# A two-layer decoder trunk: weight rounding by GpSimd copies, probability scaling by ScalarE, the first layer's gate summed by adding DMAs, and one longer list of steps

## The chip, the core and the metric

The kernel runs on one core of a Trainium2 chip. The core has a matrix engine (TensorE, PE in the profile, with its weight loads as PEld), a vector engine (VectorE, DVE), an engine for activations and scaled copies (ScalarE, ACT), a general engine (GpSimd, POOL), and a queue that mostly issues transfers (SyncE, SP). Each engine works through its own list of instructions in order and waits on semaphores for the others. The metric is the time of one execution on the device in microseconds, less is better. Three runs of the kernel before took 427.09, 427.12 and 428.16 us, median 427.12.

## The reference, cut to what matters

One sequence of 256 tokens of width 1024 passes two layers. Each layer normalizes its input, shifts and scales it with numbers computed from a conditioning vector `c`, applies a mixer, and adds the projected result back, multiplied by a gate that is also computed from `c`:

```
shift, scale, gate = split(c @ ada_w + ada_b)
x = x + gate * mixer(rmsnorm(x) * (1 + scale) + shift)
```

Layer 0 is sparse attention with 16 heads in 4 groups of keys. With 256 tokens all four blocks of 64 are selected, so the selected and the sliding branch are both plain causal attention, on different keys and values, beside a branch on 15 compressed tokens:

```
p   = exp(s - max) / sum;        s = q k^T / 8 - slope * distance
o   = g0 * o_cmp + g1 * o_slc + g2 * o_win
y   = (o * silu(z)) @ w_out
```

Layer 1 is a chunkwise mLSTM with 8 heads, followed by its own output projection and a final norm. Matrix products are made at more than one pass of reduced precision: every float32 operand is split into a rounded part (`hi`) and the remainder (`lo`), and three products hi*hi, hi*lo and lo*hi are added.

## The kernel before, in words

Weights stream from HBM through a ring of ten buffers named `raw`, 128 x 1024 floats each, always loaded on SP's queue and always in the order in which they will be used (`stream_rest`, line 935, fixes that order; a load waits until its buffer's last reader is done). A weight block is then split by two instructions: `make_hi` (line 144) rounds it into a buffer `wh` by a ScalarE copy (line 164), and `make_lo` (line 167) writes the remainder into `wl` by a VectorE subtraction (line 169). There are six pairs of `wh` and `wl`. Blocks of the attention's z path are rearranged on the way, and so take two instructions of 512 elements each for hi and again for lo.

The work has three stages. The first makes the modulated input and the query projection (line 442). The second is the one that the change rewrites: the key, value and gate-logit projections (lines 548 to 550 and 1611 to 1613), the compression network (line 581), the attention itself, the output projection (line 878, named `out_mm`), and the turn to the next layer, in which the residual is added, normalized, transposed and modulated and the first products of layer 1 begin (line 1167). The third is layer 1, whose instructions a scheduler orders.

In the second stage the order is written out by hand. The keys run as a plain loop over the eight blocks of the contraction (`nsa`, line 552), in each block all three kinds of columns. The attention follows a list of steps, `ORDER` (line 613): each word emits the instructions of one step, on whichever engines they run. There are eight units n = 0 to 7 (a pair of key groups, one head of each). `S:n,a` makes the scores of token half a on TensorE, `m:n,a` subtracts distances and takes minima on VectorE, `e:n,a` is the exponential on ScalarE with its sums, `f:n` makes the factors gate/sum on VectorE. Then the probabilities are multiplied by these factors, in eight instructions a unit (`scaled`, line 803): `p:n,j` puts four of them on GpSimd, `s:n,j` four on VectorE, `q:n,j` two on each. `T:n,j,br` transposes them on TensorE, `t:n,j,br` copies the transposes out of PSUM by ScalarE, and `V:n` multiplies by the values. `hi` and `lo` split the next weight block, `z:n,q` are the z path's products, `out:k` and the later `last` calls are the output projection, and `d:s,n` is a VectorE reduction that makes a shift or scale column of layer 1. The turn (line 1092) is straight code behind the list.

The gate of layer 0, a row of 1024 numbers, is made in the list too. `gr:n` runs 16 matmuls of `c` against 512 columns of the gate's weights, four at a time in column groups of 32 (line 226), `gc` copies the result out by ScalarE, `gs` adds the four partial rows and spreads the sum over 128 partitions by one float32 matmul (line 868), and `ga` adds it to the bias by VectorE (line 872).

## Time and profile before

| what | value |
|---|---|
| median of three runs | 427.12 us (427.09 to 428.16) |
| span of the profiled execution, first to last instruction | 425.8 us |
| median of the runs above that span | 1.3 us |
| TensorE busy | 415.7 us, 98% |
| VectorE busy | 353.7 us, 83% |
| ScalarE busy | 272.0 us, 64% |
| GpSimd busy | 82.1 us, 19% |
| granted TensorE clock, mean | 0.999 |
| moved by DMA | 94.54 MB, mean 222 GB/s |

The second stage starts at 52.7 us with the first key product and ends at about 184.8 us with the last products of the turn. A busy time is the union of an engine's instructions. TensorE's instructions overlap in the profile (one starts while the one before is still draining), so a column that says 280 ns for a matmul is not the pace: the pace is read from the starts in the timeline.

### The profile page before, as it was taken

What the parts mean: (1) busy time and instruction counts of PE and PEld (TensorE: products, weight loads), DVE (VectorE), ACT (ScalarE), POOL (GpSimd) and SP (SyncE); (2) the same over time, 40 slices, a digit from 0 to 9 for tenths busy, and PEclk for the clock granted to TensorE, in tenths of its full rate; (3) what the DMA queues carried; (4) which work ended last, traced back from release to release, by engine and by line L of the source; (5) the groups of instructions that cost most, each with busy time, mean ns of one, the idle gap of its engine ahead of it and who ended that gap; (6) DMA issues with size and microseconds to landing.
All of it is one profiled execution on the core that took longest, in us unless ns stands there. A gap on an engine that the chain in (4) does not pass through costs nothing.

```text
span 425.8 us, 7641 instructions
## 1 busy us (share of the span) xinstructions
PE 415.7 (98%) x2701; PEld 359.7 (84%) x2701; DVE 353.7 (83%) x747; ACT 272.0 (64%) x542; POOL 82.1 (19%) x127
## 2 busy tenths in 40 slices
PE   7999999999999999999999999999999999999994
PEld 4899998789778878888998899888888888888884
DVE  6999798999999998979983796889878997458553
ACT  5766693788978964668576865465456454555523
POOL 4000212364586740120000000000000350220000
PEclk9999999999999999999999999999999999999999
DMA  8999986973799678148754366558555687540002
GB/s 313 413 408 407 396 306 192 357 280 107 256 353 391 226 255 307 58 145 295 247 172 168 105 237 190 166 174 264 163 188 197 213 290 229 168 142 0 2 0 99
DMA packets 26886, 94.54 MB, mean 222 GB/s; under 512 B 3072, under 2 KB 3088, under 8 KB 26848
## 3 DMA queue, kind: packets, MB, share of 16 engines
q1 hardware_dynamic: 26208, 92.30, 61.6%
q0 software_dynamic: 352, 0.97, 0.7%
q10 hardware_dynamic: 288, 0.79, 0.5%
q8 instruction: 21, 0.34, 0.3%
q14 instruction: 17, 0.14, 0.1%
HBM read 93.00 MB, written 1.05 MB: 221 GB/s over the span
## 4 chain that ended last, share of the span: by engine, by line
PE 86%; issue 6%; DMA 2%; POOL 2%; DVE 2%; ACT 1%; SPq 1%; DVEq 0%; POOLq 0%; ACTq 0%
PE bank L550 10%; PE bank L548 10%; PE bank L549 10%; PE bank L442 8%; PE bank L1613 6%; PE bank L1611 6%; PE bank L1612 6%; PE bank L1524 5%; PE bank L1045 5%; PE bank L1167 3%; DMA Q<-in_columns 2%; PE bank L808 2%; PE bank L1404 2%; PE bank L825 2%; PE bank L763 2%
## 5 line engine op out<-in xcount | busy, mean ns | idle before, releaser
L169 DVE TENSOR_TENSOR wl<-raw,wh 128x1024 fp32r<-128x1024 f32 (+4 forms) x127 | 139.3, 1112 | 37.3 <-ACT wh L164 36.4
L164 ACT ACTIVATE wh<-raw 128x1024 fp32r<-128x1024 f32 (+4 forms) x127 | 119.4, 957 | 72.9 <-PE bank L550 31.8
L548 PE MATMUL bank<-wh,one 128*128 128x512 f32 (+1 forms) x208 | 76.8, 370 | 0.0
L549 PE MATMUL bank<-wl,one 128*128 128x512 f32 (+1 forms) x208 | 76.3, 367 | 0.0
L550 PE MATMUL bank<-wh,one 128*128 128x512 f32 (+1 forms) x208 | 76.3, 368 | 0.0
L1611 PE MATMUL bank<-one,wh 128*128 128x256 f32 x208 | 59.6, 287 | 0.0
L1613 PE MATMUL bank<-one,wl 128*128 128x256 f32 x208 | 59.2, 285 | 0.1
L1612 PE MATMUL bank<-one,wh 128*128 128x256 f32 x208 | 59.0, 284 | 0.0
L803 POOL TENSOR_SCALAR Pr<-Pr,f 128x128 f32<-128x128 f32 (+1 forms) x42 | 46.7, 1130 | 31.4 <-DVE f L797 25.1
L548 PEld LDWEIGHTS bank<-wh,one 128*128 128x128 f32 x208 | 39.2, 189 | 6.1 <-DVE tz L520 0.2
L550 PEld LDWEIGHTS bank<-wh,one 128*128 128x128 f32 x208 | 39.2, 188 | 6.1
L549 PEld LDWEIGHTS bank<-wl,one 128*128 128x128 f32 x208 | 39.2, 189 | 5.9
L1611 PEld LDWEIGHTS bank<-one,wh 128*128 128x128 f32 x208 | 39.7, 191 | 1.3 <-issue 0.8
L1613 PEld LDWEIGHTS bank<-one,wl 128*128 128x128 f32 x208 | 39.7, 191 | 0.5 <-DVE wl L169 0.3
L1612 PEld LDWEIGHTS bank<-one,wh 128*128 128x128 f32 x208 | 39.7, 191 | 0.1
L789 ACT ACTIVATE Pr<-Pr,mn 128x128 f32<-128x128 f32 (+1 forms) x64 | 28.2, 444 | 4.4 <-DVE mn L782 4.4
L442 PE MATMUL bank<-one,wh 128*128 128x256 f32 x224 | 29.8, 284 | 0.7 <-ACT one L416 0.4
L442 PEld LDWEIGHTS bank<-one,wh 128*128 128x128 f32 x224 | 28.1, 192 | 1.1 <-ACT one L416 0.6
L1487 POOL DMA_DIRECT2D DT<-in_final_g x1 | 0.6, 560 | 131.7 <-DVE pl L1399 131.7
L160 POOL TENSOR_TENSOR raw<-raw,gate 128x256 f32<-128x256 f32 x16 | 15.5, 976 | 47.8 <-DMA raw<-in_out_b 22.5
L1385 DVE SCALAR_TENSOR_TENSOR conv<-bank,one,conv 128x255 f32<-128x255 f32 (+2 forms) x48 | 20.2, 471 | 2.1 <-ACT conv L1380 2.1
L861 DVE CUSTOM_DVE_ANT_0 raw<-raw,one,one 128x1024 f32<-128x1024 f32 x16 | 21.1, 1331 | 0.0
(343 smaller groups left out, 813.6 us busy)
## 6 DMA issues: line engine op xcount, KB each, us to landing
raw<-in_wide SPq DMA_DIRECT2D x44, 512.0 KB, 4.1
raw<-in_units SPq DMA_DIRECT2D x18, 512.0 KB, 3.5
raw<-in_turn SPq DMA_DIRECT2D x16, 512.0 KB, 7.7
raw<-in_gates SPq DMA_DIRECT2D x16, 512.0 KB, 4.7
raw<-in_out_b SPq DMA_DIRECT2D x16, 512.0 KB, 3.8
raw<-in_start SPq DMA_DIRECT2D x8, 512.0 KB, 9.6
Q<-in_columns SPq DMA_DIRECT2D x8, 512.0 KB, 9.6
raw<-in_hidden SPq DMA_DIRECT2D x8, 512.0 KB, 4.2
```

The source lines that it names most:

```text
L164: self.nc.scalar.activation(v(hi), src, AF.Copy)
L169: self.nc.vector.tensor_sub(v(lo), src, v(hi).bitcast(F32))
L442: nc.tensor.matmul(out, w[:, ch * P : ch * P + P], h[:, kk], start=(kk == 0 and m == 0 and ch % 2 == 0), stop=(kk == 7 and m == 2), skip_g ...
L548: nc.tensor.matmul(out, self.hh[:, kk, sl], wh, start=first, stop=False, skip_group_check=True)
L549: nc.tensor.matmul(out, self.hh[:, kk, sl], wl, start=False, stop=False, skip_group_check=True)
L550: nc.tensor.matmul(out, self.hl[:, kk, sl], wh, start=False, stop=last, skip_group_check=True)
L789: nc.scalar.activation(v, v, AF.Exp, bias=mn[:, a, br, j : j + 1], scale=-1.0, accum_out=sm[:, a, br, j : j + 1])
L803: es[br].tensor_scalar(v, v, F[n][:, a, br, j : j + 1], None, op0=OP.mult)
L1045: ins = nc.tensor.matmul(out, l[:, sl], w[:, c0:c1], start=(k == 0 and m == 0), stop=(k == N - 1 and m == 2), skip_group_check=True)
L1611: nc.tensor.matmul(out, wh, self.hh[:, kk], start=first, stop=False, skip_group_check=skip)
L1612: nc.tensor.matmul(out, wh, self.hl[:, kk], start=False, stop=False, skip_group_check=skip)
L1613: nc.tensor.matmul(out, wl, self.hh[:, kk], start=False, stop=last, skip_group_check=skip)
```

## The change

Five things change in the second stage, and the rest only follows.

- Twenty-two of the roundings (`make_hi`) become GpSimd copies: a step `hp` in the list (`np` in the turn) does what `hi` does, on GpSimd. The z path's weights are laid out beforehand so that each block needs one copy and one subtraction instead of two of each.
- The multiplication of probabilities by their factors leaves GpSimd: of 64 such instructions 54 are ScalarE copies with a scale, and 10 stay on VectorE (steps `saa`, `sva`, `sav`, a letter for each branch).
- The gate of layer 0 no longer uses matmuls of `c`. Each of eight blocks of 128 x 1024 weights is multiplied in place by the matching column of `c` on ScalarE (`gm:k`), and a DMA issued by GpSimd adds it into the tile `gate0`, which starts as zeros with the bias in one partition (`gp`). One float32 matmul by ones for each half (`gs:n`, same size as before) then sums over the partitions, and ScalarE copies the result over `gate0` (`ga:n`).
- The keys' columns are three parts, and keys, attention and turn are one list.
- The order of the loads on SP's queue follows the new list: eight loads of one gate block each replace two groups of four.

```diff
-    def make_hi(self, m):
+    def make_hi(self, m, pool=False):
-        if kind == "z":
-            r4 = raw.rearrange("p k j (i d) -> p k j i d", i=2)
-            views = [... two of 512 elements ...]
-        elif kind == "q":
+        if kind == "q":
...
         for v, src in views:
-            self.nc.scalar.activation(v(hi), src, AF.Copy)
+            if pool:
+                self.nc.gpsimd.tensor_copy(v(hi), src)
+            else:
+                self.nc.scalar.activation(v(hi), src, AF.Copy)
...
+        self.gate0 = self.T(pc, [P, D], tag="gate")
+        g.memset(self.gate0, 0.0)
...
             if kk == 2:
+                nc.gpsimd.dma_start(self.gate0[0:1], self.t["ada_b"][0:1, 2048:3072])
...
-        def kv_block(kk):
-            wh, wl = self.take()
+        def kv_block(kk, part):
+            while len(kw) <= kk:
+                kw.append(self.take())
...
         def scaled(n, j, *es):
             for br in range(2):
                 for a in range(2):
-                    v = probs(n, j, br, a)
-                    es[br].tensor_scalar(v, v, F[n][:, a, br, j : j + 1], None, op0=OP.mult)
+                    v, f = probs(n, j, br, a), F[n][:, a, br, j : j + 1]
+                    if es[br] is nc.scalar:
+                        copy(v, v, scale=f)
+                    else:
+                        es[br].tensor_scalar(v, v, f, None, op0=OP.mult)
...
-        def rows(what, n, bank):
-            b = self.bank(bank)
-            B.setdefault("ada", []).append(b)
-            self.ada_rows(b, self.take_raw(4))
...
-        def gate_sum(bank):
-            b = B["gs"] = self.bank(bank)
-            nc.tensor.matmul(b, self.sel, W["A"].pop(0), start=True, stop=True)
+        def gate_sum(n):
+            b = B["gs"] = self.bank(4)
+            nc.tensor.matmul(b, self.ones1.to_broadcast([P, P]), self.gate0[:, 512 * n : 512 * n + 512], start=True, stop=True)
+
+        def gate_copy(n):
+            copy(self.gate0[:, 512 * n : 512 * n + 512], B["gs"])
...
+    def gate_product(self, kc):
+        raw = self.gate_raw = self.take_raw(1, True)[0]
+        self.nc.scalar.activation(raw, raw, AF.Copy, scale=self.pca[:, kc : kc + 1])
+
+    def gate_part(self):
+        self.nc.gpsimd.dma_start(self.gate0, self.gate_raw, accum_op=OP.add)
+        self.used.add(self.kept)
...
     ORDER = """
-    d:0,0 hidden:0 hi hidden:1 S:0,0 lo S:0,1 hi hidden:2 hidden:3 z:0,0 m:0,0 m:0,1 e:0,0 lo S:1,0 ...
+    k:0,1 hi qa:3 lo hi lo k:0,0 k:0,2 k:1,0 hp hi hp k:1,2 qa:1 lo lo k:1,1 k:2,1 k:2,0 hi k:3,0 k:4,0 ...
```

What the new list does to three engines' instructions is shown by pieces of their order. TensorE first: in the middle of the attention before (unit 3 and 4; `bank` tiles are PSUM banks, `raw` the weight blocks, `one_39` holds `c`, `one_16` the identity for transposes, `KH` and `KL` the split keys) the gate's matmuls stand between transposes and scores, followed by a transpose and the gate's sum.

```order
L808 MATMUL bank_1600<-one_16_87,Pr_1349 128x128 x3
L226 MATMUL bank_1615<-raw_1147,one_39_144 32x512
L226 MATMUL bank_1615<-raw_1149,one_39_144 32x512
L226 MATMUL bank_1615<-raw_1151,one_39_144 32x512
L226 MATMUL bank_1615<-raw_1207,one_39_144 32x512
...
L766 MATMUL bank_1624<-KH_758,Q_949 128x256
```

And on TensorE now, in the output projection (`wh` and `wl` are split weight blocks, `Q` the split mixer output, `gate` the tile that the DMAs add into):

```order
L896 MATMUL bank_2041<-wh_1931,Q_1000 128x512
L896 MATMUL bank_2041<-wl_1932,Q_1000 128x512
L896 MATMUL bank_2041<-wh_1931,Q_1000 128x512
L887 MATMUL bank_2271<-gate_134,one_14_85 128x512
L896 MATMUL bank_2040<-wh_2066,Q_1000 128x512
L896 MATMUL bank_2040<-wl_2067,Q_1000 128x512
```

The 16 narrow matmuls are gone from TensorE, the two sums stay, and they have moved from the middle of the attention into the output projection, behind the eighth adding DMA.

GpSimd before, in the middle of the attention (`Pr` are probabilities, `f` the factors):

```order
L803 TENSOR_SCALAR Pr_1193<-Pr_1193,f_1290 128x128
L803 TENSOR_SCALAR Pr_1193<-Pr_1193,f_1290 128x256
L803 TENSOR_SCALAR Pr_1194<-Pr_1194,f_1290 128x128
L803 TENSOR_SCALAR Pr_1194<-Pr_1194,f_1290 128x256
...
L803 TENSOR_SCALAR Pr_1348<-Pr_1348,f_1461 128x128
L803 TENSOR_SCALAR Pr_1348<-Pr_1348,f_1461 128x256
```

GpSimd now, in the same part of the program (the `wh` of `raw_1153` is the last z block, those behind it belong to the output projection):

```order
L1037 DMA gate_134<-raw_1063 128x1024
L165 CAST wh_1417<-raw_1153 128x1024
L1037 DMA gate_134<-raw_1155 128x1024
L165 CAST wh_1498<-raw_1209 128x1024
L1037 DMA gate_134<-raw_1193 128x1024
L165 CAST wh_1610<-raw_1258 128x1024
L165 CAST wh_1748<-raw_1409 128x1024
```

GpSimd's queue now alternates between the weight copies, which VectorE's subtractions and then TensorE wait for, and the adding DMAs, each of which waits for the one before it, since all write the same tile.

ScalarE now, at unit 5 and 6 (`PT` are the copied transposes, `sm` sums, `mn` minima; line 662 is the plain copy, line 818 the exponential, line 1034 the gate's product):

```order
L662 ACTIVATE PT_1922<-bank_1902 128x384
L662 ACTIVATE Pr_1783<-Pr_1783,f_1868 128x128
L662 ACTIVATE Pr_1783<-Pr_1783,f_1868 128x256
L1034 ACTIVATE raw_1480<-raw_1480,one_8_70 128x1024
L662 ACTIVATE PT_1929<-bank_1918 128x384
L662 ACTIVATE Pr_1784<-Pr_1784,f_1868 128x128
L662 ACTIVATE Pr_1784<-Pr_1784,f_1868 128x256
```

ScalarE before, between the same kinds of work:

```order
L633 ACTIVATE PT_2022<-bank_1989 128x384
L164 ACTIVATE wh_2041<-raw_1865 128x1024
L633 ACTIVATE Q_839<-y_327_1637 128x512
L164 ACTIVATE wh_2069<-raw_1867 128x1024
L633 ACTIVATE PT_2092<-bank_2012 128x384
```

Where copies of transposes stood between weight roundings, they now stand between scalings of probabilities and the gate's products.

378 lines of the change are left out of this document (164 added, 214 removed).

## The prediction

> **What bounds the kernel now.** I read the page's busy times first, then the chain that ended last, then the busy times by stage.
>
> ```profile
> PE 415.7 (98%) x2701; PEld 359.7 (84%) x2701; DVE 353.7 (83%) x747; ACT 272.0 (64%) x542; POOL 82.1 (19%) x127
> PE 86%; issue 6%; DMA 2%; POOL 2%; DVE 2%; ACT 1%; SPq 1%; DVEq 0%; POOLq 0%; ACTq 0%
> ```
>
> TensorE is busy for 98% of the span and carries 86% of the chain. So an edit counts in two ways: by what it takes off TensorE's list, and by any wait that it puts in front of TensorE. The table by stage (busy us, number of instructions in brackets, clock, DMA share, GB/s) shows where that holds. The second stage is the first five rows.
>
> ```profile
> core 0: us, PE busy (x) PEld busy (x) DVE busy (x) ACT busy (x) POOL busy (x), PEclk, DMA share, GB/s
> 52.70:80.00 27.30, 27.18 (x216) 23.63 (x216) 25.50 (x50) 19.97 (x43) 4.64 (x8) 1.00 0.78 267
> 80.00:110.00 30.00, 30.00 (x269) 25.31 (x265) 28.52 (x110) 24.58 (x81) 18.21 (x26) 1.00 0.61 224
> 110.00:140.00 30.00, 30.00 (x238) 24.54 (x235) 29.65 (x101) 24.37 (x75) 19.60 (x19) 1.00 0.92 349
> 140.00:160.00 20.00, 19.79 (x133) 15.40 (x132) 19.89 (x37) 15.85 (x36) 10.91 (x7) 1.00 0.75 239
> 160.00:184.80 24.80, 24.00 (x129) 19.74 (x128) 21.16 (x46) 13.63 (x28) 3.41 (x14) 1.00 0.48 172
> ```
>
> The stage takes 132.1 us. TensorE idles 0.12 + 0.21 + 0.80 = 1.1 us in it, at full clock. VectorE is nearly as full: from 80 to 160 us it is busy 78.06 of 80. ScalarE is busy 84.8 of the 107.3 us up to 160, so it idles 22.5. Idle by this table is not all that TensorE loses, since a matmul that starts late still overlaps its predecessor's draining. The timeline (start, duration, engine) shows both kinds:
>
> ```profile
> 55.17 0.28 PE L1611 MATMUL bank<-one,wh 128*128 128x256 f32 x1
> 55.29 0.28 PE L1612 MATMUL bank<-one,wh 128*128 128x256 f32 x1
> 55.69 0.39 PE L1613 MATMUL bank<-one,wl 128*128 128x256 f32 x1
> ...
> 181.67 0.97 PE L1167 MATMUL bank<-wh,one 128*128 128x272 f32 x5 [0.51 <-DVE one L1154]
> ```
>
> The second of these starts 0.12 us after the first, which is the usual pace, but the third 0.40 after the second, so 0.28 is lost without a gap being shown. Altogether little is lost: shortening the waits can bring one or two microseconds, and the rest must come from TensorE's work.
>
> **The change part by part.** *TensorE.* The chain in order of time has the pace of each kind of matmul (start, length, count):
>
> ```profile
> 103.55 2.75 PE bank L825 x32
> ...
> 106.82 0.48 PE bank L830 x4
> ...
> 107.59 0.68 PE bank L808 x6
> 108.28 1.85 PE bank L226 x16
> ...
> 111.13 0.98 PE bank L868 x2
> ...
> 112.44 0.92 PE bank L763 x4
> ...
> 120.06 1.85 PE bank L226 x16
> ```
>
> L226 is the gate by matmuls of `c`: two groups of 1.85 us, 3.7 us in all, and both vanish. The two sums (L868, about 0.98 us each) stay, with other operands of the same type and size. All other matmuls and transposes are the same in number and shape, only in another order. So TensorE sheds 3.7 us. For the change of neighbours (a transpose beside a product, a narrow beside a wide one) I take nothing, between -1 and +1 us.
>
> *VectorE.* These groups (count, busy us, mean ns) change:
>
> ```profile
> L803 DVE TENSOR_SCALAR Pr<-Pr,f 128x256 f32<-128x256 f32 x11 | 4.4, 400 | 0.0
> L803 DVE TENSOR_SCALAR Pr<-Pr,f 128x128 f32<-128x128 f32 x11 | 3.9, 355 | 0.1
> L872 DVE TENSOR_TENSOR gate<-gate,bank 128x512 f32<-128x512 f32 x2 | 1.3, 674 | 0.0
> L169 DVE TENSOR_TENSOR wl<-raw,wh 128x512 fp32r<-128x512 f32 x20 | 13.2, 702 | 0.0
> L169 DVE TENSOR_TENSOR wl<-raw,wh 128x1024 fp32r<-128x1024 f32 x88 | 108.3, 1236 | 37.2 <-ACT wh L164 36.4
> L169 DVE TENSOR_TENSOR wl<-raw,wh 128x816 fp32r<-128x816 f32 x10 | 10.0, 1005 | 0.1
> ```
>
> Of 22 scalings 10 stay: 6 x (0.400 + 0.355) = 4.5 us less. The two additions to the gate go: 1.3 less. The z path's 16 halves of 0.702 become 8 whole subtractions of 1.236: 11.2 - 9.9 = 1.3 less. VectorE sheds 7.2 us (4.5 + 1.3 + 1.3, before rounding). This is what makes the 3.7 us of TensorE collectable: from 80 to 160 us VectorE had only 1.9 us of idle time, less than 3.7, and would have set the pace; now it has 1.9 + 7.2 - 3.7, about 5.4.
>
> *ScalarE.* The roundings that leave it, and the nearest rows for what comes:
>
> ```profile
> L164 ACT ACTIVATE wh<-raw 128x1024 fp32r<-128x1024 f32 x88 | 92.4, 1056 | 70.2 <-PE bank L550 31.8 <-PE bank L1612 13.5 <-DMA raw<-in_start 9.1
> L164 ACT ACTIVATE wh<-raw 128x512 fp32r<-128x512 f32 x20 | 11.4, 627 | 0.8 <-DMA raw<-in_start 0.7
> L397 ACT ACTIVATE KH<-one,rq_y 128x896 f32<-128x896 f32 x1 | 1.0, 1043 | 0.1
> L789 ACT ACTIVATE Pr<-Pr,mn 128x256 f32<-128x256 f32 x32 | 15.8, 497 | 3.3 <-DVE mn L782 3.2
> L789 ACT ACTIVATE Pr<-Pr,mn 128x128 f32<-128x128 f32 x32 | 12.4, 390 | 1.2 <-DVE mn L782 1.2
> ```
>
> Off go 16 halves (16 x 0.627 = 10.0), ten blocks of 1024 (10 x 1.056 = 10.6), three of 816 and one of 544 (by length from the 1024 row, 3.1): 23.7 us. On come 54 scalings, 27 of each width. They are not in the trace; the nearest row is the exponential on the same tile with an operand per partition: 27 x (0.497 + 0.390) = 23.9 us (from below, all at the narrow price, 21.1; from above, all at the wide one, 26.8). Eight products of 1024 with such an operand come too: L397 made 896 in 1.043, so about 1.19 each, 9.5 us. The two copies out of PSUM only change their target. ScalarE gains 23.9 + 9.5 - 23.7 = 9.7 us. Its idle time up to 160 us goes from 22.5 to 22.5 - 9.7 - 3.7, about 9. This is cover, but thin, and the price when it is gone is a rival below.
>
> *GpSimd.*
>
> ```profile
> L803 POOL TENSOR_SCALAR Pr<-Pr,f 128x256 f32<-128x256 f32 x21 | 28.4, 1355 | 0.0
> L803 POOL TENSOR_SCALAR Pr<-Pr,f 128x128 f32<-128x128 f32 x21 | 19.0, 905 | 31.4 <-DVE f L797 25.1 <-PE bank L808 3.2 <-ACT PT L633 3.2
> L542 POOL CAST KH<-KH 64x512 fp32r<-64x512 f32 x4 | 2.4, 611 | 43.0 <-ACT KH L537 42.9
> L1077 POOL TENSOR_TENSOR one<-one,y 128x512 f32<-128x512 f32 x1 | 1.7, 1664 | 19.4 <-DVE y L1076 19.4
> L1487 POOL DMA_DIRECT2D DT<-in_final_g x1 | 0.6, 560 | 131.7 <-DVE pl L1399 131.7
> ```
>
> Off go 47.4 us of scaling. A rounding of 1024 elements is in no row. The cast L542 takes 0.611 for 512, so 1.22 for 1024; the slowest GpSimd row per element, L1077, would make it 3.3. I take 1.22, since it is the same operation and types: 18 x 1.22 + 3 x 0.97 + 0.65 = 25.5 us, and 8 issues of a DMA at 0.56 make 4.5. GpSimd gets lighter, at most 66 + 4.5 us by the upper price, half the stage. A copy is on no path by itself: it stands ahead of the subtraction by a step or more. The bias DMA and the memset in the first stage I cost at nothing, since GpSimd has little to do there (the fifth busy time is its own):
>
> ```profile
> 0.00:20.00 20.00, 16.59 (x123) 13.10 (x124) 15.90 (x37) 13.31 (x24) 5.89 (x33) 1.00 0.92 360
> ```
>
> *Transfers.* Gate weights stay at 4 MB. The eight adding DMAs move 4 MB more inside the chip; at the 349 GB/s of the busiest row that is 1.5 us each, 12 over a stage whose DMA share averages about 0.71: hidden as bandwidth, not always as latency (a rival). Each holds its `raw` buffer, one of ten, until it has landed, and SP's later loads with it.
>
> *Keys.* The list now runs six products a block for blocks 3 to 7 early (6 x 0.12 = 0.72 us a block), while each block needs a subtraction of 1.005 (L169, 816). TensorE has products of the first blocks to go on with, and the query remainders are moved back to make room: 0 to 1 us of waiting, taken as 0.
>
> *The sum*, made against the profiled span: 425.8 - 3.7 = 422.1. The three runs' median, 427.1, stands 1.3 above the span, so 423.4. I leave the waits as they are on balance: new ones are as likely as old ones are to go.
>
> **A rule that speaks against it.** From the trace (min/median/max in ns, by line):
>
> ```profile
> L803 POOL TENSOR_SCALAR Pr<-Pr,f x42: 598/922/2923, 81.2 to 152.1; 128x128 f32<-128x128 f32 x21, 128x256 f32<-128x256 f32 x21
> L169 DVE TENSOR_TENSOR wl<-raw,wh x127: 679/1214/1760, 11.5 to 400.3; 128x1024 fp32r<-128x1024 f32 x88, 128x512 fp32r<-128x512 f32 x20, 128x816 fp32r<-128x816 f32 x10, 128x768 fp32r<-128x768 f32 x8
> ```
>
> A GpSimd instruction that can take 0.6 us took up to 2.9 beside a full VectorE, and a subtraction stretched from about 1.21 to 1.76, so the two engines do hold each other up. If each of the 22 copies held one subtraction for its whole 1.22 us, VectorE would get 26.8 us more. Its idle time in the whole stage is 132.1 - 124.7 (the five rows) = 7.4, and 7.4 + 7.2 - 3.7 = 10.9 after the change; 15.9 would be left over, and the time 439. If each cost the most that the trace shows, 0.55, that is 12.1, 1.2 over, and the time 424.6. The Trainium skill's page "SBUF — State Buffer", section "Who interferes with whom", states the former: a VectorE instruction with two inputs in SBUF and a GpSimd instruction that reads SBUF block each other for a whole instruction. The trace agrees that they block, but 47.4 us of GpSimd work in this stage cost VectorE little, and there is less of it now; so I give the full price a small chance.
>
> **The rivals.**
>
> 1. *The waits go too.* VectorE, which the longest shown gap waits for, is relieved by 7.2 us, and the new list puts products of layer 1 between the turn's second half and its transposes. The 1.1 us of idle and about as much of hidden late starts (an estimate) go: 423.4 - 2.2 = 421.2. Against it: ScalarE is fuller. Chance 0.2.
> 2. *ScalarE takes it back.* Each unit's transposes go through two PSUM banks, and TensorE can only go on when ScalarE has copied one out. Before, a weight rounding might stand before such a copy, now four scalings, 2 x (0.497 + 0.390) = 1.77 us. If each of the eight units loses a quarter of that, 0.44, it is 3.5 us, and the time is 426.9: no change. The thin 9 us of idle time speak for it; that the scalings of a unit stand a step before its own transposes speaks against. Chance 0.13.
> 3. *The last adding DMA comes late: slower.* Each waits for the one before, and TensorE's list holds the gate's first sum, behind which the rest of the output projection is queued; ScalarE's copy and VectorE's residual wait for it in turn. Between the eighth adding DMA and that sum the new list has 15 transposes, two units of values, one compressed step and 15 wide products: 15 x 0.113 + 2.75 + 0.48 + 15 x 0.23 = 8.4 us by the chain's rows. Plain transfers of the same 512 KB land so (KB, median us):
>
> ```profile
> Q<-in_columns SPq DMA_DIRECT2D x8, 512.0 KB, 9.6
> DT<-in_final_g POOLq DMA_DIRECT2D x1, 512.0 KB, 4.9
> ```
>
> An adding one reads its target besides, so between 4.9 and twice 9.6, 19.2. It decides from 8.4 + 3.7 = 12.1 us; at 13.4 it is slower by the bound, at 19.2 the time is 423.4 + 10.8 = 434.2. I take about 8, since the queues are at 0.75 there and not full. Chance 0.1, and 0.05 for the blocking above at its full price.
>
> **How the numbers follow.** The forecast, 423.4, has 0.52 (its own range 422.0 to 425.0, from the neighbours' and the keys' microsecond); the rivals 0.2, 0.13, 0.1 and 0.05. A measurement of this kernel can tell about 0.3%, 1.3 us, from no change. The forecast and rival 1 are below 425.8: 0.72 faster; rival 2 is within: 0.13; rival 3 and the blocking, 0.15, are slower. The range goes from 420.7, a little under rival 1, to 428.0, which leaves out most of the slower 0.15 and about 0.04 below.
>
> **What would show it.** Right: no L226 of 512 columns behind 52 us, the second stage about 128.4 us long, TensorE's idle in it near 1 us, VectorE's work 7 us less, ScalarE's 10 more, GpSimd's casts at 1.2 us. Rival 2 would show as idle or late transposes behind a ScalarE copy; rival 3 as TensorE standing still before the matmul from `gate`, with the last adding DMA landing over 8 us after issue; the blocking as subtractions of 2 us and more. The forecast is wrong if the stage is not 2 us shorter, or if the third stage changes its length.

## The result, and the profile after

The changed kernel takes 432.49 us (median of 4 runs, 432.3 to 432.83) where the kernel before takes 427.35 beside it (4 runs, 427.09 to 428.16): 1.0119 times as long, 95% interval 1.0105 to 1.0133. It is slower by 5 us; the prediction said 423.4. The profiled span is 430.3 us. One kernel below (the gate alone in the old list) ran over 1.5% above its fastest execution in two of six, and its row is of the other four. First the page of the changed kernel, busy times and chain.

```profile
PE 414.1 (96%) x2669; PEld 361.2 (84%) x2669; DVE 359.1 (83%) x725; ACT 276.6 (64%) x574; POOL 69.6 (16%) x117
PE 79%; DVE 12%; ACT 5%; issue 2%; DMA 1%; POOL 0%; DVEq 0%; ACTq 0%
```

TensorE has 32 instructions less (16 narrow matmuls for each half of the gate), but VectorE, which lost 22 instructions, is busy 5.4 us longer (359.1 against 353.7), and its share of the chain has gone from 2% to 12%. The stages show where. The table by stretch of the second stage (PE, PEld, DVE, ACT, POOL busy, clock, DMA share, GB/s) answers to the five rows shown of before:

```profile
53.60:80.00 26.40, 24.80 (x189) 20.91 (x189) 25.65 (x46) 18.06 (x38) 10.90 (x12) 1.00 0.85 289
80.00:110.00 30.00, 25.08 (x212) 22.51 (x210) 29.48 (x78) 23.20 (x72) 13.25 (x19) 1.00 1.02 338
110.00:140.00 30.00, 28.72 (x247) 25.99 (x247) 29.61 (x95) 28.24 (x92) 7.04 (x7) 1.00 0.75 214
140.00:165.00 25.00, 25.00 (x171) 19.43 (x170) 23.50 (x54) 20.49 (x66) 5.84 (x5) 1.00 0.92 302
165.00:190.80 25.80, 25.25 (x139) 21.13 (x138) 21.98 (x48) 13.54 (x30) 7.26 (x18) 1.00 0.58 204
sum 137.20, PE 128.85 PEld 109.97 DVE 130.23 ACT 103.53 POOL 44.29; mean PE 25.77 PEld 21.99 DVE 26.05 ACT 20.71 POOL 8.86
```

The same stretch before, from the first key product to the last product of the turn, ends at 186.2 us, 1.4 us later than where the prediction ended the stage:

```profile
52.70:186.20 133.50, 132.37 (x983) 109.94 (x982) 125.02 (x341) 98.87 (x262) 57.62 (x73) 1.00 0.71 253
```

It is 137.2 us now, against 133.5 before, though 3.7 us of matmuls are gone. TensorE idles 8.35 us of it (137.20 - 128.85), against 1.1 (133.50 - 132.37); the clock is full throughout. What follows the stage is unchanged (239.5 us against 239.6). The time ahead of it differs by 0.9 us between the two traces; among the kernels below, whose first stage is that of the changed kernel word for word, the first key product starts anywhere from 52.4 to 54.0 us, so I read nothing into that. The waits of TensorE in the stage (us in total, times, longest) name the releasers:

```profile
PE bank L691 <- DVE y L686: 2.7, 1, 2.7
PE bank L795 <- DVE mn L811: 1.2, 1, 1.2
PE bank L730 <- ACT PT L662: 1.0, 1, 1.0
PE bank L840 <- ACT PT L662: 0.9, 1, 0.9
```

The longest is the gelu's transposes (L691). The timeline around it (start, duration, engine, and in brackets the idle time before):

```profile
82.23 0.88 POOL L1037 DMA_DIRECT2D gate<-raw  x1 [5.41 <-ACT Pr L662]
82.80 4.29 POOL L165 CAST wh<-raw 128x1024 fp32r<-128x1024 f32 x4
...
83.14 4.11 DVE L682 TENSOR_SCALAR y<-y 128x256 f32<-128x256 f32 x1
87.28 0.42 DVE L683 TENSOR_TENSOR y<-y,y 128x256 f32<-128x256 f32 x1
...
87.74 0.42 ACT L684 ACTIVATE y<-y 128x256 f32<-128x256 f32 x1 [3.20 <-DVE y L683]
...
89.43 0.30 PE L691 MATMUL bank<-one,y 128*128 128x128 f32 x1 [2.73 <-DVE y L686]
```

An instruction of 128 x 256 elements begins at 83.14 and ends at 87.25, just as GpSimd's four roundings end (82.80 + 4.29 = 87.09). In the kernel before it took 0.47 us:

```profile
L653 DVE TENSOR_SCALAR y<-y 128x256 f32<-128x256 f32 x1 | 0.5, 473 | 0.0
```

ScalarE's tanh waits for it 3.2 us, TensorE 2.7. The four roundings stand straight behind the second adding DMA, which waits until the first has landed (issued at 72.82, landed at 81.33; over all eight 5.7, 8.3 and 10.4 us from issue to landing, least, median, most). I took this wait for the reason that they ran back to back; an experiment below shows that it is not. Other VectorE groups of the stage are stretched too (count, busy us, mean ns):

```profile
L172 DVE TENSOR_TENSOR wl<-raw,wh 128x816 fp32r<-128x816 f32 x9 | 9.8, 1147 | 0.0
L682 DVE TENSOR_SCALAR y<-y 128x256 f32<-128x256 f32 x1 | 4.1, 4112 | 0.0
L835 DVE TENSOR_SCALAR Pr<-Pr,f 128x128 f32<-128x128 f32 x5 | 4.0, 796 | 0.0
L824 DVE TENSOR_SCALAR f<-sm 128x8 f32<-128x8 f32 x8 | 3.5, 433 | 0.5 <-ACT Pr L818 0.4
L752 DVE TENSOR_TENSOR tz<-tz,one 128x512 f32<-128x512 f32 x1 | 2.3, 2298 | 0.0
```

Before, the same took 1005 (816 columns), 473 (gelu), 355 (scaling), 164 (factors) and 695 ns (512 columns). VectorE does not stand and wait for the roundings themselves: before its 17 subtractions of 1024 columns it idles 0.1 us in all. So the first theory, A: GpSimd's roundings hold VectorE's instructions, worst when they run in a bunch. The rival, B: the new list and a fuller ScalarE make the waits, whoever rounds.

### The profile page after: what moved, and what is told of

It is laid out like the page before. It is cut to its first block, busy times and chain, and to the rows that moved or that the text cites. A ratio compares the mean times of both kernels' runs of the same rounds, so it can differ in the third digit from the quotient of the medians.

```text
span 430.3 us, 7590 instructions
## 1 busy us (share of the span) xinstructions
PE 414.1 (96%) x2669; PEld 361.2 (84%) x2669; DVE 359.1 (83%) x725; ACT 276.6 (64%) x574; POOL 69.6 (16%) x117
## 4 chain that ended last, share of the span: by engine, by line
PE 79%; DVE 12%; ACT 5%; issue 2%; DMA 1%; POOL 0%; DVEq 0%; ACTq 0%
PE bank L561 9%; PE bank L559 9%; PE bank L560 9%; PE bank L448 8%; PE bank L1485 5%; PE bank L1064 5%; PE bank L896 5%; PE bank L1573 4%; PE bank L1574 4%; PE bank L1572 4%; PE bank L1175 4%; ACT Pr L818 3%; DVE wl L172 2%; PE bank L1365 2%; PE bank L857 2%
## 5 line engine op out<-in xcount | busy, mean ns | idle before, releaser
L172 DVE TENSOR_TENSOR wl<-raw,wh 128x1024 fp32r<-128x1024 f32 (+3 forms) x119 | 139.8, 1190 | 35.5 <-ACT wh L167 33.1
L167 ACT ACTIVATE wh<-raw 128x1024 fp32r<-128x1024 f32 (+3 forms) x99 | 98.9, 1009 | 71.4 <-PE bank L561 31.5
L559 PE MATMUL bank<-wh,one 128*128 128x512 f32 (+2 forms) x208 | 76.7, 370 | 0.0
L561 PE MATMUL bank<-wh,one 128*128 128x512 f32 (+2 forms) x208 | 76.3, 368 | 0.0
L560 PE MATMUL bank<-wl,one 128*128 128x512 f32 (+2 forms) x208 | 76.3, 367 | 0.0
L165 POOL CAST wh<-raw 128x1024 fp32r<-128x1024 f32 (+2 forms) x20 | 25.3, 1323 | 38.3 <-PE bank L1573 16.4
L662 ACT ACTIVATE Pr<-Pr,f 128x128 f32<-128x128 f32 (+1 forms) x54 | 20.3, 449 | 3.0 <-DVE f L826 3.0
```

Of the source, the lines that this page charges most:

```text
L165: self.nc.gpsimd.tensor_copy(v(hi), src)
L167: self.nc.scalar.activation(v(hi), src, AF.Copy)
L172: (g or self.nc.vector).tensor_tensor(v(lo), src, v(hi).bitcast(F32), op=OP.subtract)
L559: nc.tensor.matmul(out, self.hh[:, kk, sl], wh, start=first, stop=False, skip_group_check=True)
L560: nc.tensor.matmul(out, self.hh[:, kk, sl], wl, start=False, stop=False, skip_group_check=True)
L561: nc.tensor.matmul(out, self.hl[:, kk, sl], wh, start=False, stop=last, skip_group_check=True)
```

## Experiments

All times are medians. The ratio is to the kernel before on the same chip, from the single executions of both, and so differs by up to 0.2% from what the medians give. Some of the expectations speak of 24 roundings on GpSimd; the trace has 22.

| kernel | us | ratio (95%) |
|---|---|---|
| the change | 432.49 | 1.0119 (1.0105 to 1.0133) |
| all roundings on ScalarE | 446.34 | 1.0449 (1.0431 to 1.0467) |
| second adding DMA moved | 430.40 | 1.0073 (1.0058 to 1.0088) |
| before, engines alone | 433.53 | 1.0142 (1.0129 to 1.0155) |
| before, gate alone | 443.20 | 1.0362 (1.0327 to 1.0396) |
| the change, matmul gate | 435.87 | 1.0192 (1.0178 to 1.0206) |
| gelu with one instruction less | 432.90 | 1.0113 (1.0093 to 1.0133) |
| short roundings | 423.36 | 0.9917 (0.9894 to 0.9939) |
| full roundings, same reads | 431.48 | 1.0098 (1.0080 to 1.0117) |
| pieces of 256 columns | 428.77 | 1.0036 (1.0018 to 1.0053) |
| pieces of 256, five DMA steps moved | 431.39 | 1.0074 (1.0051 to 1.0096) |
| pieces of 128 | 432.91 | 1.0113 (1.0095 to 1.0131) |
| pieces of 256, six on ScalarE | 444.79 | 1.0409 (1.0385 to 1.0433) |
| pieces of 128, six on ScalarE, gelu | 447.42 | 1.0462 (1.0439 to 1.0486) |
| pieces of 256, two on ScalarE | 429.25 | 1.0048 (1.0030 to 1.0066) |
| the same, second DMA moved | 430.04 | 1.0053 (1.0037 to 1.0070) |

### One part undone, or one part alone

**All roundings on ScalarE.**

```diff
-"hp": lambda: self.hi_next(True)
+"hp": self.hi_next
...
-"np": lambda n: narrow_hi(n, True)
+"np": narrow_hi
```

> The changed kernel with one thing undone: all 24 roundings that the new list gives to GpSimd in layer 1 are ScalarE copies again; the list, the gate by adding DMAs and ScalarE's scalings stay. Theory A (GpSimd's roundings block VectorE: 82.80 to 87.09 four of them ran back to back and a VectorE tensor_scalar of 0.47 us took 4.11): VectorE's instructions lose about 11 us of stretch, that tensor_scalar takes 0.47 us, and TensorE's stand of 2.9 us at 86.4 goes, with most of the smaller ones; ScalarE takes on about 24 x 0.95 = 23 us, which it has room for before 110 us and not from 110 to 140 (28.2 of 30 us busy), so 427 to 431 us. Theory B (ScalarE's queue is too full already, GpSimd's work is harmless): the stands behind ScalarE grow, nothing is gained, 435 us and more.

446.3 us: B's side of the number. But VectorE's stretches did go, as A said (the gelu's tensor_scalar takes 0.29 us, VectorE is busy 347.3 us instead of 359.1), and the table by stretch and the timeline show what took their place:

```profile
80.00:110.00 30.00, 24.84 (x207) 21.83 (x205) 23.11 (x80) 29.25 (x78) 4.51 (x11) 1.00 0.99 341
110.00:140.00 30.00, 27.68 (x232) 24.00 (x231) 24.90 (x88) 30.00 (x93) 1.72 (x2) 1.00 0.76 220
```

```profile
164.63 0.88 ACT L167 ACTIVATE wh<-raw 128x816 fp32r<-128x816 f32 x1 [4.94 <-DMA raw<-in_narrow]
165.86 0.48 PE L840 MATMUL bank<-one,Pr 128*128 128x128 f32 x1 [5.25 <-ACT Pr L662]
```

ScalarE is busy 59.25 of the 60 us from 80 to 140: the scalings have filled it, and the roundings have no room there. Later a rounding waits 4.9 us for its weight to land, with a unit's scalings queued behind it, and TensorE stands 5.25 us. In the change nothing that TensorE needs soon stands behind that rounding on GpSimd's queue (the next instruction there is at 170.22 us). So this run puts one harm in the place of another and does not settle which of them the change suffers from.

**The engines alone, in the old list.** Roundings of layer 1's list on GpSimd, GpSimd's scalings on ScalarE; the list and the matmul gate as before.

```diff
-"hi": self.hi_next
+"hi": lambda: self.hi_next(True)
...
-"p": lambda n, j: scaled(n, j, nc.gpsimd, nc.gpsimd)
+"p": lambda n, j: scaled(n, j, nc.scalar, nc.scalar)
...
-"q": lambda n, j: scaled(n, j, nc.vector, nc.gpsimd)
+"q": lambda n, j: scaled(n, j, nc.vector, nc.scalar)
```

> The kernel before with its own list and its matmul gate, and only the engines moved: the roundings of layer 1's list are GpSimd copies, and the scalings that GpSimd had are ScalarE copies. Theory A: VectorE is blocked beside the roundings here too, with no adding DMA in the queue: some VectorE instructions stretch by 1 us and more, 428 to 431 us. Theory B (the new list is what costs): no change or a little less than 427.3, as ScalarE and GpSimd only trade work.

433.5 us, 6 slower than before: more than A expected and not what B said. So in the old list the trade of engines costs by itself. The hold is not the most of it here: VectorE is busy only 1.1 us longer than before (354.8 against 353.7; single stretches reach 0.65 us), and the wait of TensorE that is longest in total is for ScalarE's copies of transposes:

```profile
PE bank L814 <- ACT PT L636: 2.8, 3, 1.1
```

That is B's fuller ScalarE in the old list. What the new list costs or saves this run cannot tell; the short roundings below can. How the 6 us divide I did not separate.

**The gate alone, in the old list.** Products on ScalarE, eight adding DMAs, evenly spread; all else as before.

```diff
-gr:0 S:4,0 T:2,1,1 y:0 gc:0 m:4,0 gs:0 ga:0
+S:4,0 T:2,1,1 y:0 m:4,0
...
+gm:0
...
+gp gm:1
...
+gs:0 ga:0 gs:1 ga:1
```

> The kernel before with its own list and engines, and only layer 1's gate made by ScalarE products and eight adding DMAs, spread evenly over the list, each DMA's step just ahead of the next product. The prediction's term alone: TensorE sheds 3.7 us of products, 423.5 us. Theory A says the same as long as nothing that is needed soon stands behind an adding DMA on GpSimd's queue; here GpSimd's scalings stand there, and a DMA that waits some 8 us for the one before it to land would hold them: 424 to 428 us. Theory B: 423.5 us.

443.2 us, far off both expectations. The stretch from 110 to 140 us, where TensorE is busy 23.1 of 30, and the wait of TensorE that is longest in total (7 times):

```profile
110.00:140.00 30.00, 23.10 (x180) 18.84 (x180) 26.62 (x90) 24.90 (x76) 19.20 (x21) 1.00 0.83 237
```

```profile
PE bank L814 <- POOL Pr L809: 5.3, 7, 1.5
```

Here GpSimd still has the scalings, and transposes that were fed in time now wait for them seven times. The scalings stand behind adding DMAs, which fits A; no run here separates this from the rest. (These 5.3 us are two fifths of the 12.7 us that the profiled execution, 440.1 us, lost; the eight products on a ScalarE that keeps its roundings are another candidate, not taken apart here.) So in the old list the gate by adding DMAs is no gain; it seems to want a GpSimd queue in which nothing is urgent.

**The gate undone in the new list.** The change with layer 1's gate by matmuls again, no adding DMAs.

```diff
-gm:3 gp gm:4 t:1,1,0
+t:1,1,0
...
-V:1 hp sav:2,1 S:4,1 t:2,0,0
+V:1 hp sav:2,1 gr:0 gc:0 S:4,1 gs:0 ga:0 t:2,0,0
...
-cpt:1 V:4 m:7,1 out:0
+cpt:1 gr:1 gc:1 V:4 gs:1 ga:1 m:7,1 out:0
```

> The changed kernel with its list, its GpSimd roundings and its ScalarE scalings, but layer 1's gate by matmuls as before: TensorE has 3.7 us of products again, ScalarE loses eight products of 1.15 us, GpSimd loses the eight adding DMAs and the waits for their landing. Theory A (the adding DMAs bunch the roundings, and the bunch blocks VectorE): the bunch of four at 82.8 is gone and with it 2 to 3 us of stands, which pays for most of the 3.7 us: 432 to 434 us. Theory B (the stands come with the list and the roundings alone): 432.5 + 3.7 = 436 us.

435.9 us: B's number, 3.4 slower than the change (3.1 by the ratios). So in this list the new gate brings nearly the 3.7 us of the prediction's first term, and A's expectation that the bunch would pay most of it back was too hopeful: with no DMA issue ahead of the roundings the gelu's tensor_scalar took 1.18 us, but other waits came (1.3 us before the compressed scores, 1.2 before the second group of gate products).

### One step moved, one instruction folded

**The second adding DMA behind the four roundings.**

```diff
-gelu:0 gp hp hp m:1,0
+gelu:0 hp hp m:1,0
...
-f:1 z:0,0 hp turned gm:2
+f:1 z:0,0 hp turned gp gm:2
```

> The changed kernel with one step moved: the second adding DMA goes behind the four roundings that stood behind it on GpSimd's queue. In the trace it waited until 81.36 for the first adding DMA to land (issued 72.82, landed 81.33), and the four roundings then ran back to back from 82.80 to 87.09, beside the 4.11 us tensor_scalar. Theory A (the held queue bunches the roundings, the bunch blocks VectorE): the roundings spread out from about 77 us on, the tensor_scalar takes under 2 us, TensorE's stand of 2.9 us at 86.4 shrinks below 1 us, 429.5 to 431 us. Theory B (the stand belongs to the new list itself, whoever runs the roundings): the stand stays, 432.5 us.

430.4 us, 2.1 less than the change, as A said. TensorE's wait for the gelu went from 2.7 to

```profile
PE bank L691 <- DVE y L686: 1.2, 1, 1.2
```

and the tensor_scalar from 4.11 to 1.18 us. One step of a table of hundreds, and no instruction more or less. But the roundings did not spread out from 77 us on, as I had expected:

```profile
81.05 3.07 POOL L165 CAST wh<-raw 128x1024 fp32r<-128x1024 f32 x3 [5.32 <-PE bank L561]
82.04 1.18 DVE L682 TENSOR_SCALAR y<-y 128x256 f32<-128x256 f32 x1
```

Three still run back to back. They wait for TensorE to free a `wh` buffer, and with the gate by matmuls, with no adding DMA at all, they start at 81.12. So it was not the wait of the DMA that bunched them. What differs is that no DMA issue stands straight ahead: VectorE's instruction now gets through after one rounding. All in all VectorE is busy almost as long as in the change (358.3 us against 359.1): about the same hold, spread over other instructions, costs 2.1 us less.

**The gelu with one VectorE instruction less.**

```diff
-nc.scalar.activation(h2, h1, AF.Square)
+nc.scalar.activation(h2, h1, AF.Square, scale=0.044715**0.5)
...
-nc.vector.tensor_scalar(h2, h2, 0.044715, 1.0, op0=OP.mult, op1=OP.add)
-nc.vector.tensor_tensor(h2, h2, h1, op=OP.mult)
+nc.vector.scalar_tensor_tensor(h2, h2, 1.0, h1, op0=OP.add, op1=OP.mult)
```

> The changed kernel with one VectorE instruction less: the cube's factor goes into the scale of ScalarE's square, and the tensor_scalar (0.47 us alone, 4.11 beside the four roundings) and the product after it become one scalar_tensor_tensor. Same result up to rounding. Theory A, with every VectorE instruction that works in the state buffer held alike: the new instruction starts at about 83.1 and is held until the last of the four roundings ends near 87.1, the stand at 86.4 shrinks by no more than the 0.4 us that left the chain: 432 us. Theory A', in which only the instruction that was there was held for the whole of the four and one with two inputs gets through after one rounding (the subtractions were held about 0.7 us): about 1 us in place of 4.5, and 429.5 to 430.5 us.

432.9 us, no change, as A said. The new instruction was held as the old one:

```profile
81.96 4.79 DVE L682 SCALAR_TENSOR_TENSOR y<-y,y 128x256 f32<-128x256 f32 x1
```

So it is not a matter of one kind of instruction (A', with its 429.5 to 430.5, falls).

### The length of the roundings

**Short roundings, and full ones with the same reads.** In the first GpSimd converts 32 columns of each weight instead of all; in both, the products and VectorE's subtraction take column 0 of the rounding in place of the rounded weight. The subtraction takes the same column away that the product adds, so the weights' products are less exact, and not left out as the first text says: the remainder is the size of the weight itself and rounded once.

```diff
-self.nc.gpsimd.tensor_copy(v(hi), src)
+self.nc.gpsimd.tensor_copy(hi[:, 0:32], src[:, 0:32])
...
+hi = hi[:, 0:1].to_broadcast([P, 1024])
```

> The changed kernel with the same list, steps, buffers and waits, but each of GpSimd's 24 roundings in layer 1's list converts 32 of its columns instead of up to 1024; the products and VectorE's subtractions read column 0 in place of all of them, so these weights' products are left out of what is computed. Theory A (roundings on GpSimd block VectorE): the tensor_scalar of 4.11 us takes 0.47, VectorE's other stretches of 0.5 to 2 us go except those beside a DMA issue, TensorE's stand of 2.9 us at 86.4 goes and most of the smaller ones: 432.5 less 4 to 7 us, 425 to 428. Theory B (the list and ScalarE's queue cost it): 431 to 432.5.

> The counterpart of the kernel with the short roundings: the same products and subtractions that read column 0 of GpSimd's roundings, but the roundings convert all their columns again. (The subtraction takes the same column away that the product adds, so the weights' products are less exact and not left out; the words of the run with the short roundings say otherwise.) If the 9 us between the changed kernel and that run come from the length of GpSimd's roundings, this one takes what the changed kernel takes, 431 to 433 us. If they come from operands that are read with a step of zero, it takes what that run took, 423 to 424 us.

423.4 and 431.5 us. This is the experiment that decides: with the same list, the same waits and the same ScalarE work, the length of GpSimd's roundings is worth 8.1 us (7.7 by the ratios), more than A had expected, and without it the kernel takes about what the prediction said. That it is the prediction's number within 0.1 us is luck: the span of the profiled execution is 421.1 us where the sum had 422.1, and its time stands 1.9 us above the span where the sum took 1.3. With short roundings, the page, the sum of the stretches from 53.6 to 182 us, and the gelu's tensor_scalar in the timeline:

```profile
PE 411.4 (98%) x2669; PEld 359.8 (85%) x2669; DVE 346.5 (82%) x725; ACT 276.1 (66%) x574; POOL 54.3 (13%) x117
```

```profile
sum 128.40, PE 126.56 PEld 108.87 DVE 117.33 ACT 103.61 POOL 28.66; mean PE 25.31 PEld 21.77 DVE 23.46 ACT 20.72 POOL 5.73
```

```profile
81.69 0.29 DVE L684 TENSOR_SCALAR y<-y 128x256 f32<-128x256 f32 x1
```

VectorE is 12.6 us less busy than in the change (346.5 against 359.1), ScalarE within 0.5 us the same. TensorE's idle in the stage falls from 8.35 to 1.84 us. The start of the same TensorE instruction in the two timelines tells where the stage falls back:

| instruction of the change | the change | short roundings | behind by |
|---|---|---|---|
| score product, L795 | 73.67 | 72.25 | 1.42 |
| gelu's transpose, L691 | 89.43 | 85.00 | 4.43 |
| compressed scores, L730 | 99.05 | 93.86 | 5.19 |
| score product, L795 | 110.35 | 103.68 | 6.67 |
| transpose, L840 | 134.81 | 126.78 | 8.03 |
| a product of the turn, L1175 | 184.13 | 175.06 | 9.07 |

A third of the loss comes between the first two rows, all of it at the gelu (4.43 - 1.42 = 3.01); the rest is spread, some tenths to 1.5 us at a time.

### The hold, measured by itself

Behind the last work of the changed kernel six VectorE instructions of 128 x 256 f32 run alone, and then beside six GpSimd roundings of 128 x 1024, in one execution.

```diff
+for w in ws[:casts]:
+    nc.gpsimd.tensor_copy(w, a)
+for o in os:
+    kind(o)
```

> The changed kernel with a measurement behind its last work (the time is longer by it and is not compared): six VectorE instructions of one kind on 128 x 256 f32, first alone and then beside six back-to-back GpSimd roundings of 128 x 1024, for a tensor_scalar, a tensor_tensor, a scalar_tensor_tensor and a copy out of the state buffer, and a tensor_scalar and a tensor_tensor that read a PSUM bank. Theory A: one or more of the kinds that work in the state buffer alone is held for the whole run of roundings (about 6 us), as the 0.47 us tensor_scalar was for 4.11 us. Theory B: beside the roundings each kind takes less than 0.3 us longer than alone, or each waits once for one rounding, about 1 us.

The groups of each, alone and then beside (count, least, median and most ns): a tensor_scalar, a tensor_tensor, and a tensor_tensor with one operand in PSUM.

```profile
L258 DVE TENSOR_SCALAR one<-one x6: 278/282/285, 433.2 to 434.2; 128x256 f32<-128x256 f32 x6
L258 DVE TENSOR_SCALAR one<-one x6: 295/1120/1127, 435.7 to 440.1; 128x256 f32<-128x256 f32 x6
L259 DVE TENSOR_TENSOR one<-one,one x6: 416/418/426, 443.2 to 444.9; 128x256 f32<-128x256 f32 x6
L259 DVE TENSOR_TENSOR one<-one,one x6: 426/1252/1257, 446.5 to 451.5; 128x256 f32<-128x256 f32 x6
...
L263 DVE TENSOR_TENSOR one<-bank,one x6: 414/414/425, 485.5 to 487.2; 128x256 f32<-128x256 f32 x6
L263 DVE TENSOR_TENSOR one<-bank,one x6: 411/414/425, 488.3 to 490.0; 128x256 f32<-128x256 f32 x6
```

Out of the state buffer (SBUF, where all tiles but the PSUM banks lie) the two engines take turns, one VectorE instruction for one rounding: each waits 0.84 us (1.120 - 0.282; 1.252 - 0.418). The copy and the scalar_tensor_tensor do the same; with a PSUM operand and one in the state buffer nothing is lost. This is the rival's second case, about 1 us once for each rounding. It explains the many stretches of 0.7 to 1.2 us, and it does not explain 4.11 us. The Trainium skill's page "SBUF — State Buffer", section "Who interferes with whom", says that the two engines block each other for a whole instruction; these rows agree, with 0.84 us for what is left of a rounding.

**The same behind a DMA issue.** What differed in the kernel was the DMA issue straight ahead of the roundings.

```diff
+add = lambda: nc.gpsimd.dma_start(d, a, accum_op=OP.add)
+plain = lambda: nc.gpsimd.dma_start(d, a)
...
+(ts, lambda: (add(), casts(4, 1024))),
+(tt, lambda: (add(), casts(4, 1024))),
+(ts, lambda: (plain(), casts(4, 1024))),
+(ts, add),
+(ts, lambda: casts(4, 256)),
...
```

> The measurement behind the changed kernel's last work once more, with other neighbours of the six VectorE instructions (128 x 256 f32): an adding DMA issue and four roundings of 1024 columns behind it (tensor_scalar, then tensor_tensor); a plain DMA issue and four roundings; an adding DMA issue alone; sixteen roundings of 256 columns (tensor_scalar, then tensor_tensor); an adding DMA issue and sixteen short roundings. Theory A, second part: behind a DMA issue one VectorE instruction is held for all four roundings, about 4 us, as the 4.11 us one in the changed kernel; without it they take turns. Rival: turns are taken there too, 1.1 us each, and the 4.11 us have another cause. Short roundings: 0.5 us for each VectorE instruction in place of 1.12.

In that order (the tensor_tensor with short roundings and the adding DMA with short ones are not shown):

```profile
L258 DVE TENSOR_SCALAR one<-one x6: 279/279/4661, 433.0 to 438.4; 128x256 f32<-128x256 f32 x6
L259 DVE TENSOR_TENSOR one<-one,one x6: 413/414/4859, 440.5 to 446.6; 128x256 f32<-128x256 f32 x6
L258 DVE TENSOR_SCALAR one<-one x6: 280/281/4406, 448.9 to 454.0; 128x256 f32<-128x256 f32 x6
L258 DVE TENSOR_SCALAR one<-one x6: 273/279/408, 456.1 to 457.2; 128x256 f32<-128x256 f32 x6
L258 DVE TENSOR_SCALAR one<-one x6: 479/480/497, 462.2 to 464.2; 128x256 f32<-128x256 f32 x6
```

Behind a DMA issue there are no turns: one instruction is held for all four roundings, 4.4 to 4.9 us, whether the DMA adds or not; the issue alone costs 0.13 us. Here no wait for another DMA is shown ahead of the issue, so it is the issue straight ahead that does it. Why, the runs do not show; the roundings overlap each other more behind an issue (in the change each of the four is 1.34 to 1.36 us long, with the DMA's step moved the first three are 1.04 to 1.10, and both start 0.98 us apart). Short roundings without a DMA cost 0.2 us each (480 - 282). Behind an adding DMA sixteen short roundings let VectorE take turns (478 ns) in this measurement, but not always in the kernel, as the next part shows.

### Versions

**Pieces of 256 columns; the same with five DMA steps moved behind the roundings.**

```diff
-self.nc.gpsimd.tensor_copy(v(hi), src)
+for c in range(0, n, w):
+    self.nc.gpsimd.tensor_copy(v(hi)[:, c : c + w], src[:, c : c + w])
```

> The changed kernel with each GpSimd rounding of layer 1's list cut into pieces of 256 columns (272 of 816 and 544), nothing else. In the measurement behind the kernel, VectorE's instructions out of the state buffer took turns with the roundings, one instruction for one rounding: 282 ns alone, 1.12 us beside roundings of 1024 columns. Theory A (a turn is one GpSimd instruction): a piece of 256 columns holds VectorE for about 0.25 us, the stretches of 0.7 to 1.2 us shrink to 0.2 to 0.4, and only those behind a DMA issue stay: 427 to 430 us. Theory B (what counts is how long GpSimd works in all): 432.5 us or more, as the pieces add their own starts.

> The kernel with the cut roundings, and five of the adding DMAs' steps moved behind the roundings that followed them at once, so that no rounding starts straight behind a DMA issue. Theory A with its second part (behind a DMA issue the roundings follow without a gap and VectorE gets no turn until the last): 424.5 to 427.5 us, below the kernel before. If the DMA issue has no part in it: as the kernel with the cut roundings alone.

The pieces win back 3.7 us, 428.8, as A said; the tensor_scalar of the gelu takes 0.29 us. Moving five DMA steps on top loses 2.6 again (1.6 by the ratios, whose intervals just touch), against the expectation: TensorE's waits behind ScalarE's copies and scalings are longer in it by 1.6 us together (3.1 against 1.5). Nor does the edit do all that its expectation says: a DMA that it left in place is issued at 139.42, twelve pieces follow straight behind it, and a tensor_scalar of 128 x 8 is held for 1.84 us among them. I have no single cause for the rest; moving more than one step of the list changes too much at once.

**Pieces of 128 columns.** As above with `w` 128.

> The changed kernel with each GpSimd rounding of layer 1's list in pieces of 128 columns (136 of 816 and 544) in place of the 256 of the run that took 428.8 us. If what is left of the loss is the length of a turn, it halves again: 426 to 428 us. If each turn has a fixed price, or the pieces' own starts on GpSimd count, it stays or grows: 428.5 to 431 us.

432.9 us, above both expectations: the gain is gone. VectorE's subtractions in the stage, with pieces of 256 and then of 128 (count, busy us, mean ns, idle time before and its releaser):

```profile
L175 DVE TENSOR_TENSOR wl<-raw,wh 128x1024 fp32r<-128x1024 f32 x18 | 23.6, 1317 | 1.8 <-POOL wh L168 1.5 <-ACT wh L170 0.3
```

```profile
L175 DVE TENSOR_TENSOR wl<-raw,wh 128x1024 fp32r<-128x1024 f32 x17 | 21.3, 1257 | 5.6 <-POOL wh L168 5.6
```

The subtractions are held less (1257 ns against 1317), but VectorE now stands 5.6 us, where it stood 1.5, until a rounding is finished at all. My reading, not shown by a run of its own, is that GpSimd must win a turn for each of eight pieces, and that the price has moved from VectorE's instructions to the roundings' end. Part of what this execution lost is the clock: 2.8 of the 5.0 us that it falls behind the pieces of 256 come between 99.4 and 105.5 us, where the granted clock is 0.52.

**Some roundings on ScalarE.** Six of them (the two ahead of the scores, the four of the turn); the six with pieces of 128 and the folded gelu; the two alone; the two and the second adding DMA moved.

```diff
-k:1,0 hp hi hp k:1,2
+k:1,0 hi hi hi k:1,2
...
-"np": lambda n: narrow_hi(n, True)
+"np": narrow_hi
```

> The kernel with pieces of 256 columns (428.8 us), and six of the 24 roundings back on ScalarE: the two ahead of the scores, at 56 to 60 us, and the four in the turn, where ScalarE was busy 18 of 26 and 13 of 26 us. Beside the kernel with short roundings the one with pieces falls back 1.8 us by 74 us and 0.8 us in the turn. If these are VectorE's turns with the six, and ScalarE has room there: 426.5 to 428 us. If ScalarE has no room in its queue after all (all 24 there took 446 us): 428.5 to 431 us.

> Both together, pieces of 128 columns and the six roundings on ScalarE, and the tensor_scalar of the gelu folded into ScalarE's square as in the earlier run. If the gains of the turns' length and of the six add up: 424.5 to 427 us, below the kernel before at 427.5. If only one of them is real: 427 to 429 us.

444.8 and 447.4 us, 13.8 and 18.4 us above the highest that was expected. The table by stretch and the timeline of the first show two stands:

```profile
90.00:96.00 6.00, 6.00 (x33) 6.00 (x33) 4.81 (x12) 6.00 (x17) 5.85 (x15) 0.58 1.00 399
152.00:162.00 10.00, 2.46 (x17) 1.62 (x12) 5.67 (x10) 2.58 (x7) 0.00 (x0) 0.73 1.04 351
162.00:167.00 5.00, 4.94 (x17) 3.77 (x19) 0.00 (x0) 3.25 (x11) 0.00 (x0) 0.52 0.48 193
```

```profile
160.83 0.88 ACT L170 ACTIVATE wh<-raw 128x816 fp32r<-128x816 f32 x1 [7.42 <-DMA raw<-in_narrow]
```

From 153 us on ScalarE waits 7.42 us for a weight of the turn, with scalings behind it: not a lack of room, but a wait put into a queue that others need. TensorE stands 7.6 us. At 86 it stands 4.1 us: sixteen pieces ran straight behind the second adding DMA and held the gelu's tensor_scalar for 5.44 us. By the start times of the same instruction in the kernel with pieces of 256 alone, the later stand costs about 13 us with what follows it in the turn, the one at 86 about 4.

> The kernel with pieces of 256 columns (428.8 us), and only the two roundings ahead of the scores on ScalarE. With six there it took 444.8, and its trace shows two stands of TensorE: 4.1 us at 86, where sixteen pieces ran straight behind the second adding DMA's issue and held the gelu's tensor_scalar for 5.44 us, and 7.6 us at 152, where ScalarE waited 7.4 us for a weight to land with a unit's scalings queued behind it; up to 70 us it was 0.6 us ahead. If the 7.6 us belong to the four in the turn, they are gone here. If the 4.1 us belong to the two early ones (GpSimd is free earlier and its pieces queue up behind the adding DMA), they stay: 432 us. If they were chance: 428 us.

> The same with the second adding DMA's step moved behind the four roundings that followed it (that step alone won 2.1 us with whole roundings). If a run of roundings straight behind a DMA issue is what holds VectorE, the tensor_scalar takes under 1 us and the stand at 86 goes: 427 to 428.5 us, about the kernel before. If not: as the run beside it.

With the four of the turn back on GpSimd it is 429.3, no better than with all of them there (428.8), and with the DMA moved 430.0, above its expectation. The stand at 86 is gone in both (the tensor_scalar takes 0.29 us): in the first the pieces start 1.25 us after the DMA issue's end, since they wait for a free buffer. So the stand hung on whether the pieces came straight behind the issue, and moving the DMA had nothing left to win.

No version here that keeps the roundings exact is faster than the kernel before; pieces of 256 columns come to 0.2 to 0.5% above it. Short roundings are below it (0.9917), but with less exact products, so I do not count them as a replacement.

## Why the prediction was wrong

The terms that make the kernel faster were right. The step that failed is what the copies on GpSimd do to VectorE: the sum gives it nothing ("a copy is on no path by itself"), and the rule that speaks against it lets VectorE's idle time absorb it, so that 12.1 us of hold would cost 1.2. Measured, 12.6 us of hold cost TensorE 8 to 9.

- **TensorE sheds 3.7 us**: right. The gate undone in the new list costs 3.4 us; with short roundings TensorE's busy time is 4.3 us below the kernel before.
- **VectorE sheds 7.2 us**: right as work, 353.7 - 346.5 = 7.2 with short roundings; in the change it gained 5.4, since 12.6 us of being held came on top.
- **ScalarE gains 9.7 us**: over-sized. 272.0 became 276.6. The prices were right (0.502 and 0.396 us for a scaling, 1.15 for a product), but neighbours overlap: four scalings of 1.80 us together take 1.50 in the timeline. With 0.1 us for each of 32 instructions more (an estimate from these), that is 3 of the 5 us; the rest I did not trace. Rival 2 did not occur as put: no transposes late at each unit.
- **GpSimd's roundings at 1.22 us and DMA issues at 0.56**: near enough for the roundings (mean 1.33 in the stage); the issue of an adding DMA takes 0.87. Wrong was "a copy is on no path by itself": it holds VectorE, which is.
- **The transfers, and rival 3**: the eighth adding DMA landed 9.8 us after issue, before TensorE wanted the sum, 13.3 us after the issue (163.40 - 150.11) and not the 8.4 that I had added up; rival 3 did not occur. But I asked of the adding DMAs only what they hold in SP's loads, not what their issue does to the instructions behind it on GpSimd's queue: the four roundings became one hold.
- **Keys at 0**: right without the hold (TensorE waits 0.4 us up to the first scores); with it the first scores come 1.4 us later.
- **The rule that speaks against it**: the step that failed. I took 0.55 us for each of 22 roundings, the most that a subtraction of the kernel before was stretched by, and set the sum, 12.1 us, against VectorE's idle time. In total 12.1 was nearly what came, 12.6, but by luck: it is not 22 equal holds but one of 3.8 us, others of 0.4 to 1.6, and most subtractions are not held at all. The waits of VectorE in the kernel before were no bound: measured, a turn is 0.84 us and a bunch behind a DMA issue 4 to 5. What failed is the idle time. The 12.6 us of hold cost TensorE 8 to 9, while VectorE still idles 7.0 us of the stage (137.20 - 130.23). What counts is which instruction is held; the gelu's was on the path to TensorE.
- **Waits "as they are on balance"**: wrong for the same reason; with short roundings it held (1.84 us of idle, near the 1.1 of before).
- **Full price of the blocking, 439, at 0.05**: the right mechanism, with too small a chance and too high a price, since not every rounding meets an instruction that it can hold. Its sign, subtractions of 2 us and more, came for one subtraction only (2.05 us); the long holds fell on other instructions. The time lay between my two prices for it, 424.6 and 439, and the range should have reached into that.

## What to carry to other kernels

Before work is moved to GpSimd, list the VectorE instructions that work in the state buffer alone at that place: each can be held for the whole GpSimd instruction beside it, and what matters is whether TensorE waits for that one, not VectorE's idle time. Do not put a run of GpSimd work straight behind a DMA issue on its queue, as the whole bunch can then be one hold. A wait that is harmless at the head of an idle engine's queue is expensive at the head of a busy one's: four roundings whose wait cost TensorE nothing that I could see on GpSimd cost some 13 us on ScalarE.

## What the runs showed of the hardware that I had not expected

- Behind a DMA issue of GpSimd, four roundings held one VectorE instruction for 4.4 to 4.9 us, where without the issue each rounding lets one through after 0.84 us.
- After TensorE stood for 4.1 and for 7.6 us (the version with six roundings on ScalarE) the granted clock was 0.58 from 90 to 96 us and 0.52 from 162 to 167, so such a stand is paid again; after the 2.7 us stand of the change it was 1.00. The Trainium skill's page "TensorE: Matmul & The Clock Gate", Part 1, gives half speed after an idle window of about 3.4 us; these rows agree. But the length of one stand does not settle it: with pieces of 128 the clock was 0.52 from 100 to 106 though no stand was longer than 2.3 us (TensorE was busy 1.64 of the 4 us from 96 to 100), and with the gate alone in the old list it was 0.50 from 86 to 89.2 after a stand of 1.7 us (busy 1.31 of the 3 us from 83 to 86).
